# Seven products of halves in place of eight for five more FFN block pairs, with the weight sums made one by one in one buffer

## The chip, the core and the metric

The kernel runs on one core of one Trainium2 chip. The metric is the device time of one execution in microseconds (us); the time before is the median of three runs. One further execution was taken with the hardware profiler, and every duration below is from that one.

Five engines appear in the profile: PE (TensorE, the matmuls, with PEld, its weight loads, shown apart), DVE (VectorE), ACT (ScalarE), POOL (GpSimd) and SP (here only the queue from which transfers are started).

## What is computed

A two-layer decoder trunk for 512 tokens of width 1024: an RG-LRU mixer, a gated conv-FFN, an RWKV-7 mixer, a second conv-FFN and a final norm. The change touches the two FFNs alone. Each computes

```python
def _conv_ffn(x, norm, w_up, conv_w, conv_b, w_down):
    h = _rmsnorm(x, norm)
    u = jnp.einsum('btd,df->btf', h, w_up)              # 512 x 1024 times 1024 x 6144
    gate = _causal_dwconv(u[..., :D_FF], conv_w, conv_b)   # 3 taps, D_FF = 3072
    hid = jax.nn.gelu(gate, approximate=True) * u[..., D_FF:]
    return jnp.einsum('btf,fd->btd', hid, w_down)          # 512 x 3072 times 3072 x 1024
```

All data are float32. The kernel writes each float32 operand as a rounded high part and a low rest and makes every product from three matmuls (high by high, high by low, low by high): this is `mm3`, line 49.

## The kernel before, in words

**Blocks, pairs, stages.** The 3072 hidden channels are 24 blocks of 128, taken in 12 pairs n = 0 to 11. A pair has gate columns G and up columns U, 256 each. Every pair reads four pieces of up weights of 512 KB (512 rows by 256 columns: the upper and the lower half of the rows for G and for U). `ffn` (line 556) goes through the pairs in the order 0, 1, 2, ... After each odd pair from 3 on, `down` (line 784) multiplies four finished hidden blocks with their four pieces of down weights (eight blocks after pair 11). I call an even pair, the odd pair behind it and the down product a *stage*: pairs 2 and 3, 4 and 5, and so on to 10 and 11.

**Two ways to make a pair.** `Whole` (line 665) makes four products, G0, U0, G1, U1: for one half of the rows, 2 column blocks x 4 row blocks x 3 = 24 matmuls with 512 moving columns (all the tokens). `Halves` (line 694) cuts the tokens into two halves of 256 and the rows into two halves, and gets the 2 x 2 block product from seven products in place of eight (Strassen's scheme in Winograd's form). Its products are numbered 1, 5, 6, 2, 7 and then 4, 3; each is 24 matmuls with 256 moving columns. The moving sums (`operands`, line 603) are made once per FFN. The sums of weights are made for each pair, by DVE, in `Halves.weights` (line 698): f[5] = f[7] + f[4], f[6] = f[5] - f[1], f[7] = f[1] - f[7], f[3] = f[6] - f[2], where f[1], f[7], f[4], f[2] are the four pieces as they were loaded.

**Before a product can run**, its weights are split: ACT rounds the piece or sum into a high part (line 93 for Whole and for down pieces, line 711 for Halves) and DVE subtracts (line 96, line 712). A Whole pair has four splits; a Halves pair has seven, and four sums. `ahead` (line 758) keeps the Halves splits two products ahead of the product that is running; `next_weights` (line 177) keeps the other splits two pieces ahead.

**After the products**, results leave the accumulators: for Whole at lines 682 and 688, for Halves at lines 730 (ACT) and 732 to 743 (DVE). `gate` (line 650) applies the convolution (ACT 656, DVE 658 twice for each block) and the gelu (ACT 659); the hidden block is split again (lines 748 to 750, or `split`).

**Which pairs are Halves**: 3, 5, 7, 9, 11 in both FFNs (`HALVES`, line 31). So each of the stages has an even Whole pair and an odd Halves pair.

**Buffers.** All pieces, sums and split parts come from one pool of `N4` = 21 buffers of 4 KB per partition (`b4`, line 83). Eight of them hold the FFN's input in high and low parts (`norm_block`, line 291, through `pair`) for the whole FFN; 13 are left for weights. A buffer is reused when its last reader is done. The framework places every semaphore and, within each engine, may order ready instructions by its own plan, with the written order as the priority; each engine then runs its own list in order.

**Loading.** `weights_load` starts the transfers from SP's queue in the order of the plan (line 99): the up pieces of a stage's pairs, then its four down pieces. They start as buffers come free. For a Halves pair behind a Whole one, line 773 asks for its four pieces just after the even pair's G0.

**Inside a stage** the order on PE is: the even pair; products 1, 5, 6, 2, 7 of the odd pair; the first down piece; products 4 and 3; the second down piece; then `then()`, which calls `ahead` for the next stage; then the third and fourth down pieces together.

Of the kernel before, what the change touches and what calls it, by code (L numbers as in the profile page):

```python
# [7 lines left out]
F32 = mybir.dt.float32  # L8
F32R = mybir.dt.float32r
AF = mybir.ActivationFunctionType  # L10
ALU = mybir.AluOpType
# [16 lines left out]
WARM2 = 20  # L28
WARM = 14

HALVES = (3, 5, 7, 9, 11)

PARAMS = [
    [("lru_b_in", 16), ("lru_conv_w", 32), ("lru_conv_b", 8),
# [9 lines left out]
class Kernel:  # L44
# [54 lines left out]
    def plan_weights(self):  # L99
        I = self.I  # L100
        plan = []
        self.quads = []

        def add(w, r0, c0, k=2, quad=False):
            plan.append((w[r0 : r0 + k * P, c0 : c0 + D // k].rearrange("(k p) c -> p k c", p=P), k, quad))

        def full(w, groups, rows=8):
            for g in groups:
                for k in range(0, rows, 2):
                    add(w, k * P, g * 512)  # L110

        def ffn(l):
            up, dn = I["ffn_w_up"][l], I["ffn_w_down"][l]

            def gu(six):


                for n in range(2 * six, 2 * six + 2):
                    self.quads.append(len(plan))
                    i = int(n in HALVES)  # L120
                    for half, r in ((i, 0), (1 - i, 0), (0, 512), (1, 512)):
                        add(up, r, half * DFF + n * 256, 4, bool(i))

            def dd(row, n):
                for g in range(2):
                    for k in range(0, n, 2):
                        add(dn, row + k * P, g * 512)

            gu(0)
            for six in range(1, 6):  # L130
                gu(six)
                if six < 5:
                    dd((six - 1) * 512, 4)
            dd(2048, 8)

        full(I["lru_w_in"][0], [2, 3, 0, 1])
        full(I["lru_w_out"][0], [0, 1])
        ffn(0)
        for i in (1, 0):
            full(I["rwkv_w_rkv"][0, i], [0, 1])  # L140
        for g in range(4):
            for k in range(0, 8, 4):
                add(I["rwkv_w_rkv"][0, 2], k * P, g * 256, 4)
        for h in range(2):
            for g in range(4):
                add(I["rwkv_w_out"][0], h * 512, g * 256, 4)
        ffn(1)
        self.plan = plan
        self.loaded, self.splitted = {}, {}
        self.n_load = self.n_split = self.n_used = 0  # L150
# [405 lines left out]
    def ffn(self, l, xs, finish, after=None):  # L556
        nc, tc = self.nc, self.tc
        last = l == 1
        with tc.tile_pool(name=f"ffn{l}", bufs=1) as pool:
# [21 lines left out]
            def start(c):  # L581
                if c == 0:
                    norm.append(self.norm_end(rbs))
                    next(norm[0])
                elif c == 1:
                    next(norm[0])
                    if last:
                        self.push(by_tokens())
# [14 lines left out]
            def operands():  # L603
                n1, t2, t3, t4 = sums

                def parts(t, k, f):
                    nc.scalar.copy(t[:, 0, k], f)
                    nc.vector.tensor_tensor(t[:, 1, k], f, t[:, 0, k].bitcast(F32), ALU.subtract)

                stt = nc.vector.scalar_tensor_tensor  # L610
                for k in range(4):
                    x1, x2 = self.x[:, k, :], self.x[:, 4 + k, :]
                    d, f = two(t("s", 7)), two(t("s", 7))
                    nc.scalar.mul(d[:, 0], x1[:, H:], gain(k))
                    stt(d[:, 1], x1[:, 0:H], gain(k), d[:, 0], ALU.mult, ALU.subtract)
                    parts(n1, k, d[:, 1])
                    stt(f[:, 0], x2[:, H:], gain(4 + k), d[:, 1], ALU.mult, ALU.add)
                    parts(t2, k, f[:, 0])
                    stt(f[:, 1], x2[:, 0:H], gain(4 + k), f[:, 0], ALU.mult, ALU.subtract)
                    parts(t4, k, f[:, 1])  # L620
                    stt(d[:, 1], x2[:, H:], gain(4 + k), d[:, 0], ALU.mult, ALU.subtract)
                    parts(t3, k, d[:, 1])
                op = {i: [tuple(part[:, h] for part in xs[k + k0][:2]) for k in range(4)]
                      for i, k0, h in ((1, 0, slice(0, H)), (2, 4, slice(0, H)), (3, 4, slice(H, T)))}
                for i, v in ((5, n1), (6, t2), (7, t3), (4, t4)):
                    op[i] = [(v[:, 0, k], v[:, 1, k]) for k in range(4)]
                return op
# [14 lines left out]
            tt = nc.vector.tensor_tensor  # L642
# [22 lines left out]
            class Whole(Pair):  # L665
                order = (("G0", "U0", "G1", "U1"), ())

                def weights(pair, p):
                    pass
# [24 lines left out]
            class Halves(Pair):  # L694
# [3 lines left out]
                def weights(pair, p):  # L698
                    if p == 1:
                        i = quads[pair.n]  # L700
                        self.weights_load(i + 4)
                        pair.f = dict(zip((1, 7, 4, 2), [self.loaded.pop(i + j) for j in range(4)]))
                    f = pair.f
                    if p == 1:
                        f[5], f[6], f[3] = (self.b4(F32, (4, 256), name) for name in ("S1", "S2", "S4"))
                        tt(f[5], f[7], f[4], ALU.add)
                        tt(f[6], f[5], f[1], ALU.subtract)
                        tt(f[7], f[1], f[7], ALU.subtract)
                        tt(f[3], f[6], f[2], ALU.subtract)
                    hi, lo = self.b4(F32R, (4, 256), f"hi{p}"), self.b4(F32R, (4, 256), f"lo{p}")  # L710
                    nc.scalar.copy(hi, f[p])  # L711
                    tt(lo, f[p], hi.bitcast(F32), ALU.subtract)  # L712
                    pair.w[p] = hi, lo
# [37 lines left out]

            quads = self.quads[l * 12 : l * 12 + 12]
            pairs, hids = {}, []
            kind = lambda n: Halves if n in HALVES else Whole
            seq = [(n, p) for n in range(12) for part in kind(n).order for p in part]
            made, at = [0], [0]

            def ahead(j):
                while made[0] < min(j, len(seq)):
                    n, p = seq[made[0]]  # L760
                    if n not in pairs:
                        pairs[n] = kind(n)(n)
                    pairs[n].weights(p)
                    made[0] += 1

            def products(upto, more=2):

                while True:
                    n, p = seq[at[0]]
                    at[0] += 1  # L770
                    ahead(at[0] + more)
                    pairs[n].product(p)
                    if p == "G0" and n + 1 in HALVES:
                        self.weights_load(quads[n] + 8)
                    if n == 0 and p in ("G0", "U0"):
                        start(int(p == "U0"))
                    if n == 1 and p == "U0":
                        op.update(operands())
                    if p == 7:
                        self.weights_split(quads[n] + 6)  # L780
                    if (n, p) == upto:
                        return
# [57 lines left out]
            for n in range(3, 12, 2):  # L840
                products((n, 7))
                if n == 11 and not last:
                    self.norm_begin()
                    self.push(self.lora_weights())
                down(n, 2 * n - 6, 4 if n < 11 else 8, lambda: products((n, 3)), lambda: ahead(at[0] + 2))
# [879 lines left out]
```

## Time and profile before

| | us |
|---|---|
| median of three runs | 1303.51 (1301.37 to 1304.6) |
| the profiled execution, its own time | 1306.19 |
| its span, first to last instruction | 1304.5 |
| PE busy | 1282.5 |
| DVE busy | 961.5 |
| ACT busy | 666.2 |

The first FFN lies at about 158 to 528 us of the span, the second at about 908 to 1298. In views of the timeline a row gives the start, the length and the instruction (`x24` are 24 merged instructions). In the view by windows each engine has its busy time in that stretch with the count of instructions in brackets; then come the granted TensorE clock, the share of the transfer engines and GB/s. Busy time of PE is of pipelined matmuls whose ends are modelled, so the pace is read from the starts of successive products.

### The profile page before, as it was taken

The numbers are of one execution on the slowest core, as the hardware profiler recorded it, in microseconds if no ns is written. First come the engines' busy times: TensorE is split into PE (matmuls) and PEld (weight loads), VectorE is DVE, ScalarE is ACT, GpSimd is POOL, SyncE is SP. The second block draws the span as 40 slices with busy tenths as digits, with TensorE's granted clock in tenths as the row PEclk, the third lists the DMA queues.
The fourth block names the chain that finished last, engine by engine and source line by source line (L and its number), as shares of the span: only waits on it lengthen the run. The fifth ranks groups of instructions, "written<-read, shape, count | busy, mean of one in ns | idle before, by whom it ended". The sixth has DMA issues, their size and how long they took to land.

```text
span 1304.5 us, 22295 instructions
## 1 busy us (share of the span) xinstructions
PE 1282.5 (98%) x9267; PEld 1077.8 (83%) x9267; DVE 961.5 (74%) x1448; ACT 666.2 (51%) x1064; POOL 67.2 (5%) x114
## 2 busy tenths in 40 slices
PE   9999999999999999999999999899999999999997
PEld 8877888988888888776678788778889898988886
DVE  5988778767667677698889975768777676766754
ACT  6897454433434344468744567655645343433432
POOL 4000000000000000010001121110000000000000
PEclk9999999999999999999899999999999999999999
DMA  6323340515050513422203111222314141505131
GB/s 196 117 65 98 97 134 29 162 33 166 28 177 21 174 50 93 153 65 92 81 23 100 43 53 58 69 83 81 100 62 131 64 146 48 164 31 173 35 132 65
DMA packets 96709, 120.40 MB, mean 92 GB/s; under 512 B 9498, under 2 KB 70628, under 8 KB 96480
## 3 DMA queue, kind: packets, MB, share of 16 engines
q1 hardware_dynamic: 95248, 117.20, 28.5%
q8 instruction: 72, 1.18, 0.4%
q10 hardware_dynamic: 576, 1.05, 0.2%
q0 software_dynamic: 784, 0.74, 0.2%
q14 instruction: 29, 0.24, 0.1%
HBM read 114.44 MB, written 4.52 MB: 91 GB/s over the span
## 4 chain that ended last, share of the span: by engine, by line
PE 87%; DVE 8%; ACT 3%; issue 1%; POOL 0%; POOLq 0%; DVEq 0%; ACTq 0%
PE acc L53 27%; PE accU L53 12%; PE accG L53 12%; PE accA L53 8%; PE accF L53 4%; PE acc L807 3%; PE acc L806 3%; PE acc L805 3%; PE accD L53 2%; PE lg L53 1%; DVE X L1248 1%; DVE wl L96 1%; PE s L1366 1%; PE lwa L53 1%; DVE DA L1246 1%
## 5 line engine op out<-in xcount | busy, mean ns | idle before, releaser
L93 ACT CAST wh<-raw 128x1024 fp32r<-128x1024 f32 (+1 forms) x161 | 166.1, 1043 | 202.9 <-PE acc L53 53.0
L96 DVE TENSOR_TENSOR wl<-raw,wh 128x1024 fp32r<-128x1024 f32 (+1 forms) x161 | 194.3, 1214 | 98.2 <-ACT wh L93 82.9
L53 PE MATMUL accG<-xs,wh 128*128 128x512 f32 x448 | 138.7, 391 | 0.0
L53 PE MATMUL accU<-xs,wh 128*128 128x512 f32 x448 | 138.6, 391 | 0.0
L53 PE MATMUL acc<-hid,wh 128*128 128x512 f32 x384 | 119.7, 395 | 0.0
L53 PEld LDWEIGHTS accG<-xs,wh 128*128 128x128 f32 x448 | 83.7, 188 | 17.3
L53 PEld LDWEIGHTS accU<-xs,wh 128*128 128x128 f32 x448 | 83.6, 188 | 17.1
L53 PE MATMUL accG<-xs,wl 128*128 128x512 f32 x224 | 87.3, 390 | 0.0
L53 PE MATMUL accU<-xs,wl 128*128 128x512 f32 x224 | 87.3, 390 | 0.0
L53 PEld LDWEIGHTS acc<-hid,wh 128*128 128x128 f32 x384 | 71.2, 188 | 16.9 <-ACT wh L93 0.4
L53 PE MATMUL accA<-xt,hi 128*128 128x256 f32 x480 | 83.4, 277 | 0.0
L53 PE MATMUL acc<-xs,wh 128*128 128x512 f32 x256 | 80.2, 394 | 0.0
L658 DVE SCALAR_TENSOR_TENSOR cv<-gpad,pv,cv 128x512 f32<-128x512 f32 x96 | 69.0, 747 | 12.3 <-ACT cv L656 11.8
L712 DVE TENSOR_TENSOR lo<-raw,hi 128x1024 fp32r<-128x1024 f32 x40 | 48.3, 1219 | 40.2 <-PE accU L53 40.2
L807 PE MATMUL acc<-wl,hid 128*128 128x512 f32 (+1 forms) x200 | 77.2, 386 | 0.0
L806 PE MATMUL acc<-wh,hid 128*128 128x512 f32 (+1 forms) x200 | 77.0, 385 | 0.0
L805 PE MATMUL acc<-wh,hid 128*128 128x512 f32 (+1 forms) x200 | 76.7, 383 | 0.0
L53 PE MATMUL acc<-hid,wl 128*128 128x512 f32 x192 | 74.9, 395 | 0.0
L53 PEld LDWEIGHTS accA<-xt,hi 128*128 128x128 f32 x480 | 73.2, 188 | 0.9
L711 ACT CAST hi<-raw 128x1024 fp32r<-128x1024 f32 x40 | 42.0, 1051 | 57.7 <-PE accG L53 49.6
L53 PE MATMUL accA<-xt,lo 128*128 128x256 f32 x240 | 66.3, 276 | 0.0
L53 PE MATMUL acc<-mix,wh 128*128 128x512 f32 x192 | 60.3, 399 | 0.0
(411 smaller groups left out, 3012.9 us busy)
## 6 DMA issues: line engine op xcount, KB each, us to landing
raw<-in_ffn_w_up_dram SPq DMA_DIRECT2D x96, 512.0 KB, 3.6
raw<-in_ffn_w_down_dram SPq DMA_DIRECT2D x48, 512.0 KB, 3.8
raw<-in_rwkv_w_rkv_dram SPq DMA_DIRECT2D x24, 512.0 KB, 3.9
raw<-in_lru_w_in_dram SPq DMA_DIRECT2D x16, 512.0 KB, 3.8
raw<-in_lru_w_out_dram SPq DMA_DIRECT2D x8, 512.0 KB, 3.8
raw<-in_rwkv_w_out_dram SPq DMA_DIRECT2D x8, 512.0 KB, 3.4
xd<-x SPq DMA_DIRECT2D x8, 256.0 KB, 2.1
AR<-xd SPq DMA_DIRECT2D x1, 2048.0 KB, 8.8
```

The costliest lines, as they stand in the source:

```text
L53: mm = lambda *a, **kw: self.nc.tensor.matmul(ps, *a, skip_group_check=more, **kw)
L93: put = (self.nc.vector.tensor_copy if dve else self.nc.scalar.copy)(hi, src)
L96: self.nc.vector.tensor_tensor(lo, src, hi.bitcast(F32), ALU.subtract)
L658: nc.vector.scalar_tensor_tensor(cv, pair.gp[:, e, j : j + T], cw(j), cv, ALU.mult, ALU.add)
L711: nc.scalar.copy(hi, f[p])
L712: tt(lo, f[p], hi.bitcast(F32), ALU.subtract)
L805: nc.tensor.matmul(ps, hh[:, s], wh[:, k, m], start=kk == 0, stop=False)
L806: nc.tensor.matmul(ps, hl[:, s], wh[:, k, m], start=False, stop=False)
L807: nc.tensor.matmul(ps, hh[:, s], wl[:, k, m], start=False, stop=kk == blocks - 1)
L1246: nc.vector.tensor_tensor(w, A[:, s + 1 :, s : s + 1].to_broadcast([P, n, j]), X[:, s : s + 1, 0:j].to_broadcast([P, n, j]), ALU.mult)
L1248: nc.vector.tensor_tensor(X[:, s + 1 :, 0:j], X[:, s + 1 :, 0:j], w, ALU.add)
L1366: nc.tensor.matmul(pss[h][half(z), b, col], w, AR[H][half(h), b, c2, q * P + col.start : q * P + col.stop], start=True, stop=True, tile_po ...
```

## The change

- `HALVES` becomes one set for each FFN. In the first FFN pair 10 becomes a Halves pair. In the second FFN pairs 4, 6, 8 and 10 do, so that all from 3 on are Halves.
- The sums of weights are no longer all made with product 1. f[5] and the new f[7] are made with product 5, f[6] with product 6, f[3] with product 3. f[5], f[6] and f[3] are one buffer ("S"), overwritten in place; three buffers become one.
- The four pieces of an odd Halves pair are asked for after the even pair's product 5, where that is a Halves pair too.
- The first two down pieces are asked for and split after product 7 only where no Halves pair of the same stage follows.

```diff
-HALVES = (3, 5, 7, 9, 11)
+HALVES = ((3, 5, 7, 9, 10, 11), (3, 4, 5, 6, 7, 8, 9, 10, 11))
...
-                    i = int(n in HALVES)
+                    i = int(n in HALVES[l])
...
                     f = pair.f
-                    if p == 1:
-                        f[5], f[6], f[3] = (self.b4(F32, (4, 256), name) for name in ("S1", "S2", "S4"))
+
+                    if p == 5:
+                        f[5] = f[6] = f[3] = self.b4(F32, (4, 256), "S")
                         tt(f[5], f[7], f[4], ALU.add)
+                        tt(f[7], f[1], f[7], ALU.subtract)
+                    if p == 6:
                         tt(f[6], f[5], f[1], ALU.subtract)
-                        tt(f[7], f[1], f[7], ALU.subtract)
+                    if p == 3:
                         tt(f[3], f[6], f[2], ALU.subtract)
...
-            kind = lambda n: Halves if n in HALVES else Whole
+            kind = lambda n: Halves if n in HALVES[l] else Whole
...
-                    if p == "G0" and n + 1 in HALVES:
+                    if p in ("G0", 5) and n + 1 in HALVES[l] and n % 2 == 0:
                         self.weights_load(quads[n] + 8)
...
-                    if p == 7:
+                    if p == 7 and (n % 2 or n + 1 not in HALVES[l]):
                         self.weights_split(quads[n] + 6)
```

## The prediction, made before the changed kernel was timed

> **What bounds the kernel now.** I read the page first: which engine is busy, and on which engine the chain that ended last lies.
>
> ```profile
> span 1304.5 us, 22295 instructions
> PE 1282.5 (98%) x9267; PEld 1077.8 (83%) x9267; DVE 961.5 (74%) x1448; ACT 666.2 (51%) x1064; POOL 67.2 (5%) x114
> PE 87%; DVE 8%; ACT 3%; issue 1%; POOL 0%; POOLq 0%; DVEq 0%; ACTq 0%
> ```
>
> PE is busy for 98% and carries 87% of the chain; but an average can hide stages with other limits. So next the view by windows, cut at the FFNs, and its last window, where PE has nothing to do.
>
> ```profile
> 158.10:528.00 369.90, 369.90 (x2035) 319.93 (x2034) 272.47 (x353) 158.29 (x205) 1.94 (x1) 1.00 0.32 101
> 908.20:1298.00 389.80, 389.46 (x2160) 338.02 (x2159) 262.16 (x338) 163.01 (x221) 4.25 (x5) 1.00 0.30 96
> 1298.00:1304.50 6.50, 0.00 (x0) 0.00 (x0) 1.16 (x4) 1.23 (x3) 0.66 (x1) 0.62 0.22 82
> ```
>
> In both FFNs PE (the first busy figure) is never idle for long, at full clock. Here PE's own work is the time, and only a change of PE's work, or a wait put in front of it, moves the end. The pace is read from the chain in order of time, for pairs 6 and 7 of the second FFN.
>
> ```profile
> 1084.66 5.44 PE accG L53 x24
> 1090.11 5.44 PE accU L53 x24
> 1095.55 5.44 PE accG L53 x24
> 1100.98 5.44 PE accU L53 x24
> 1106.42 2.87 PE accA L53 x24
> 1109.30 2.74 PE accF L53 x24
> 1112.04 2.72 PE accA L53 x24
> 1114.76 2.86 PE accD L53 x24
> 1117.62 2.74 PE accA L53 x24
> ...
> 1125.85 2.75 PE accA L53 x24
> 1128.60 2.86 PE accF L53 x24
> ```
>
> Pair 6 (Whole) takes 4 x 5.44 = 21.76 us of PE. Pair 7 (Halves) takes 2.87 + 2.74 + 2.72 + 2.86 + 2.74 + 2.75 + 2.86 = 19.54 us. No product waits for anything between them.
>
> **The change part by part.** *PE's work.* Five pairs go from Whole to Halves: 5 x (21.76 - 19.54) = 5 x 2.22 = 11.1 us less, all on the path. A half-width matmul starts every 2.74 / 24 = 114 ns and a full one every 5.44 / 24 = 227 ns, so halving costs almost nothing per column, and 7/8 of the work shows as 0.90 of the time.
>
> A rule that speaks against this is in the Trainium skill, page "TensorE: Matmul & The Clock Gate", section "Back-to-back issue gap": with a weight load ahead of each matmul it gives a sustained spacing of about 81 ns at 128 columns and 131 ns at 512. By a straight line between these (an estimate, some 98 ns at 256) a Whole pair would take 96 x 131 ns = 12.6 us and a Halves pair 168 x 98 ns = 16.4 us, and the change would cost 5 x 3.8 = 19 us. The fence above has both products of this kernel timed, at 227 and 114 ns, so the trace decides against that rule and it gets no chance below.
>
> *DVE's work.* What a pair needs, from the groups in the window of that stage (count, busy, mean ns):
>
> ```profile
> L96 DVE TENSOR_TENSOR wl<-raw,wh 128x1024 fp32r<-128x1024 f32 x9 | 11.0, 1223 | 11.6 <-ACT wh L93 7.8 <-PE acc L806 3.7
> L658 DVE SCALAR_TENSOR_TENSOR cv<-gpad,pv,cv 128x512 f32<-128x512 f32 x8 | 5.7, 747 | 0.9 <-ACT cv L656 0.9
> L712 DVE TENSOR_TENSOR lo<-S,hi 128x1024 fp32r<-128x1024 f32 x3 | 3.7, 1222 | 0.3 <-ACT hi L711 0.2
> L709 DVE TENSOR_TENSOR S<-S,raw 128x1024 f32<-128x1024 f32 x1 | 1.2, 1225 | 0.0
> L688 DVE TENSOR_TENSOR s<-accU,ge 128x512 f32<-128x512 f32 x2 | 1.4, 686 | 0.0
> L739 DVE TENSOR_TENSOR gpad<-accA,rb 128x512 f32<-128x512 f32 x1 | 0.7, 692 | 0.7 <-PE accA L53 0.7
> L711 ACT CAST hi<-raw 128x1024 fp32r<-128x1024 f32 x4 | 4.2, 1048 | 6.6 <-PE accG L53 5.8 <-DVE lo L712 0.8
> ```
>
> Whole: 4 splits x 1.22 + 4 x 0.75 (658) + 6 narrow ones x 0.69 = 12.0 us. Halves: 7 splits and 4 sums, 11 x 1.22, + 4 x 0.75 + 9 x 0.69 = 22.6 us. So each changed pair adds 10.6 us to DVE. ACT gains 3 casts of 1.05 and some copies, at half load. Is there room on DVE?
>
> ```profile
> 458.30:528.00 69.70, 69.70 (x386) 60.02 (x386) 53.96 (x66) 31.41 (x40) 0.00 (x0) 1.00 0.30 88
> 1084.70:1148.00 63.30, 63.30 (x361) 55.59 (x360) 42.87 (x51) 24.95 (x30) 0.00 (x0) 1.00 0.32 100
> 180.00:191.00 11.00, 11.00 (x50) 9.12 (x49) 10.93 (x21) 6.12 (x14) 0.00 (x0) 1.00 0.31 98
> 191.00:202.00 11.00, 11.00 (x51) 9.09 (x49) 10.69 (x26) 6.93 (x15) 0.00 (x0) 1.00 0.60 191
> ```
>
> A stage of the second FFN has DVE busy 42.9 of 63.3 us (third busy figure); after, 53.5 of 61.1, 88%. The first FFN's last stage goes from 54.0 of 69.7 to 64.6 of 67.5, 96%. The last two rows show that DVE at 98% does not by itself hold PE, where what it does is not due at once. But inside a stage the load is uneven: the two pairs up to the odd pair's product 7 give DVE 22.6 + 7 splits and sums (8.5) + 3 narrow (2.1) + two down splits (2.4) = 35.6 us in 33.5 us of PE (19.54 + 13.93), of which two products' splits (6 us) are done ahead. About 30 us in 33.5: it fits, with little to spare, and tightest about the end of the even pair, where its gate and hidden work (7 us) meets the odd pair's sums.
>
> *The sums moved.* Same four instructions; two buffers fewer per pair. Sum 6 overwrites sum 5, so on DVE it waits for ACT's cast of sum 5 (1.05) and the split behind it; what is queued behind on DVE is the splits of products 6 and 2. Two products of lead (5.6 us) cover that chain of 1.22 + 1.05 + 1.22 + 1.22 + 1.05 + 1.22 = 7.0 us for two products; without lead it would cost 1.4 us a pair. I take 0 (bounds 0 and 1.4).
>
> *Loads moved.* The odd pair's four loads are asked for at product 5 of the even one; behind them in SP's queue stand the down pieces. The transfers are the same. What may come late is the first down piece, since buffers free up later:
>
> ```profile
> 1111.81 1.23 DVE L712 TENSOR_TENSOR lo<-S,hi 128x1024 fp32r<-128x1024 f32 x1 [0.20 <-ACT hi L711]
> 1112.00 0.37 SPq L157 DMA_DIRECT2D raw<-in_ffn_w_down_dram  x1
> 1115.87 1.05 ACT L93 CAST wh<-raw 128x1024 fp32r<-128x1024 f32 x1 [0.49 <-DMA raw<-in_ffn_w_down_dram]
> 1116.95 1.22 DVE L96 TENSOR_TENSOR wl<-raw,wh 128x1024 fp32r<-128x1024 f32 x1 [3.91 <-ACT wh L93]
> 1120.81 0.37 SPq L157 DMA_DIRECT2D raw<-in_ffn_w_up_dram  x1
> 1125.66 1.05 ACT L93 CAST wh<-raw 128x1024 fp32r<-128x1024 f32 x1 [2.38 <-PE acc L806]
> 1126.74 1.23 DVE L96 TENSOR_TENSOR wl<-raw,wh 128x1024 fp32r<-128x1024 f32 x1 [2.21 <-ACT wh L93]
> 1137.35 1.40 DVE L810 SCALAR_TENSOR_TENSOR xtok<-acc,rs,xtok 128x512 f32<-128x512 f32 x2
> ```
>
> The first load started 5.6 us into the odd pair, when its second product ended and gave a buffer back. Its split was done at 1118.2, 2.2 us ahead of need (1120.4). After, the odd pair's seven splits are made beside its products and no longer ahead of them (before, the last, the first row, was through at 1113.0). By counting the 13 buffers through both pairs I get that load some 2 to 3 us later, so 0 to 0.8 us of waiting a stage, plus what DVE's crowding adds. I take 0.6 us for each of the four stages of the second FFN and 1.2 for the crowded one of the first (bounds 0 and 2.2): 4 x 0.6 + 1.2 = 3.6 us.
>
> *The sum.* 11.1 - 3.6 = 7.5 us less. The profiled execution, 1306.19 us, would be 1298.7; it lies 2.7 above the median 1303.5, so the median becomes 1296.0. About 0.3% (3.9 us) is what a measurement of this kernel can tell from no change.
>
> **The rivals.** *B, DVE becomes the bound at the seam of the two pairs.* From the even pair's product 3 to the odd pair's product 6, 8.5 us of PE, DVE has 7 us of gate and hidden work and splits and sums of products 5 and 6 (three sums and two splits, 6.1 us): 13.1 us. If only two products of lead are there (5.6 us), some 3 us of it spent by ACT's steps in between, the shortfall is 13.1 - 8.5 - 2.6 = 2.0 us a pair. For it: the 88%. Against it: the 7 us can be put off, since these hidden blocks are wanted only by the next stage's down product; and the rows at 98%. Price: of 2.22 won a pair 1.2 to 2.2 are lost, the upper end with the first down piece's wait; 5 x 0.02 to 5 x 1.0 = 0.1 to 5 us are won: 1298.4 to 1303.4.
>
> *C, slower: buffers run out ahead of the fourth down piece.* In the written order `then()` prepares the next even pair ahead of the fourth down piece's split. Before, `then()` had nothing to do (a Whole pair came next) and that split ran at 1126.74, 10 us early, in the two buffers that the first down piece had just left (the cast waits for L806). Now the next pair's four pieces, its first split parts and its sum compete for these: two parts of the third piece, the fourth piece, four up pieces, two parts, a sum, two parts and the two parts in question are 14, and there are 13. If the fourth piece's parts must wait until the second down piece is through, cast 1.05 + split 1.22, and up to four results of DVE in front at 0.70 (1.40 for two), make 5.1 us, of which six matmuls of the third piece (6 x 0.23 = 1.4) are cover: PE waits 0.9 to 3.7 us. It decides from 2.2 us on. Full price: 5 x (3.7 - 2.2) = 7.5 us slower, 1311.0. Against it: the plan is free to split the fourth piece first while the up pieces are still on their way.
>
> For waits this long the Trainium skill (same page, section on the HAM clock gate) says that a window of about 3.4 us without PE work halves the clock; the row of 6.5 us without PE work shows 0.62. By that rule each wait of 3.7 us might cost up to 1.7 us more, and C would end near 1319; my price leaves it out.
>
> *D, the change takes no time from PE* because a Halves pair behind another runs slower. But products 7, 4 and 3 above run behind others of their kind at 2.74 to 2.86 us; at 2.87 for all seven the gain is 1.67 a pair, within the forecast's range. It gets no chance of its own.
>
> **How the numbers follow.** Forecast (11.1 less 0 to 1.2 us a pair, 1292.4 to 1298.4): 0.58. B: 0.24. C: 0.18. Below 1299.6 is faster: all of the forecast and 0.10 of B, 0.68. Within 0.3% (to 1307.4): 0.14 of B and 0.06 of C, 0.20. Slower: 0.12 of C. The range starts at 1291 (no waits at all, less the spread of the runs, 1.5) and reaches to 1306, which leaves out most of C's upper part.
>
> **What would show it.** Right: 15 Halves pairs in place of 10, three copies at L730 and seven casts at L711 for each, the even pairs' products at 2.72 to 2.87 us, a stage of some 61.5 us, PE busy down by about 11, DVE near 53 of 61. B would show as PE waiting for L712 around the seam, C as PE waiting for L96 at the third and fourth down pieces. I am wrong if stages 4 to 10 of the second FFN are longer than 63 us, or if a product of an even Halves pair takes over 3 us without a wait.

## The result: slower, 1325.0 us, and the profile after

The changed kernel takes 1325.03 us (median of 4 runs, 1323.99 to 1326.30) against 1304.05 of the kernel before: a ratio of 1.0169, 95% interval 1.0152 to 1.0185 (the two medians alone give 1.0161). The forecast was 1296.0 (1291 to 1306), so it missed by 29 us and in its sign. The profiled execution is 1325.41 us long, its span 1323.7. In the kernel after, lines from 705 on stand three lower than before (L711 is now L714, L730 is L733, L806 is L809).

The page of the kernel after, span and busy times:

```profile
span 1323.7 us, 23107 instructions
PE 1280.3 (97%) x9627; PEld 1086.9 (82%) x9627; DVE 1006.8 (76%) x1498; ACT 687.4 (52%) x1094; POOL 68.6 (5%) x114
```

VectorE's load rose by 45 us, where 5 x 10.6 = 53 was the forecast. PE's busy time fell by only 2.2 us, not 11, although it does the shorter work. The view by windows says why. Columns are the span of the window, busy time of PE, weight loads, VectorE, ScalarE and GpSimd, the granted clock, DMA share and GB/s:

```profile
158.10:528.00 369.90, 364.41 (x2083) 317.26 (x2083) 276.10 (x356) 158.90 (x207) 1.94 (x1) 1.00 0.31 97
908.90:1317.20 408.30, 392.06 (x2449) 349.44 (x2447) 298.50 (x377) 180.04 (x245) 4.24 (x5) 0.97 0.28 92
1074.44:1077.90 3.46, 0.02 (x1) 0.02 (x1) 3.46 (x5) 1.99 (x2) 0.00 (x0) 1.00 0.00 0
1077.90:1084.70 6.80, 6.35 (x14) 4.58 (x15) 6.12 (x7) 1.61 (x2) 0.00 (x0) 0.50 0.00 0
1146.20:1153.03 6.83, 4.84 (x11) 3.34 (x12) 6.74 (x9) 2.55 (x3) 0.00 (x0) 0.50 0.00 0
1217.88:1224.71 6.83, 5.64 (x14) 4.13 (x13) 5.20 (x6) 2.09 (x2) 0.00 (x0) 0.50 0.00 0
```

The first row is the first FFN, where PE is now idle for 5.5 us (before 0). The second row is the second FFN: before, PE was idle for 0.3 us there at clock 1.00; now it is idle for 16.2 us at clock 0.97. The third and fourth rows are one place of it. PE does nothing for 3.46 us, and for the 6.80 us behind that it runs at a clock of 0.50. Such a wait occurs three times, ending at 1077.9, 1147.8 and 1216.9, and each has one stretch at half clock near its end. The stretches do not begin with the end of the wait each time: the second (fifth row) begins 1.56 us ahead of it, while PE still stands, and the third (last row) 0.94 us behind it. What a stretch costs is half of the time that PE worked in it: (6.35 + 4.84 + 5.64) / 2 = 8.4 us in all. The sum of the second FFN: 16.2 us idle and 8.4 us of lost clock are 24.6 us. From its first product to the end of the span it takes 414.8 us (before 396.4); the clean gain of four pairs, 4 x 2.22, and those 24.6 us give 412.1. The last 2.7 us I can't assign; short waits come out too short, since the ends of matmuls are modelled.

What PE waited for, by the view of waits of the kernel after (us in all, times, longest; one of the five waits of the second row lies ahead of the second FFN, the rest in it):

```profile
PE acc L808 <- ACT wh L93: 11.5, 4, 3.6
PE accA L53 <- ACT s L733: 3.4, 5, 0.7
PE acc L810 <- DVE wl L96: 2.1, 3, 1.2
```

The first row is the third down piece: PE stands at its first matmul until ScalarE has cast it. The last row is its low part, for which PE stands again a few matmuls later; the second row is product 4, which waits for the copy of product 7's result. ScalarE's and then VectorE's timeline ahead of the stop at 1077.90 (start, duration, instruction, in brackets the idle time before it and what ended it):

```profile
1066.70 1.53 ACT L656 ACTIVATE cv<-gpad,pv 128x512 f32<-128x512 f32 x2 [7.57 <-DVE gpad L742]
...
1070.91 1.03 ACT L714 CAST hi<-raw 128x1024 fp32r<-128x1024 f32 x1
1072.23 1.23 ACT L752 CAST hid<-s 128x512 fp32r<-128x512 f32 x2 [0.29 <-DVE s L751]
1075.84 1.04 ACT L714 CAST hi<-S 128x1024 fp32r<-128x1024 f32 x1 [2.38 <-DVE S L707]
1076.79 1.04 ACT L93 CAST wh<-raw 128x1024 fp32r<-128x1024 f32 x1
```

```profile
1073.38 1.21 DVE L715 TENSOR_TENSOR lo<-raw,hi 128x1024 fp32r<-128x1024 f32 x1
1074.51 1.22 DVE L707 TENSOR_TENSOR S<-raw,raw 128x1024 f32<-128x1024 f32 x1
```

The cast of the third piece (L93) needs no input that is late: the four down pieces' loads were all issued by 1057.2. It starts without a gap behind the cast of sum S (L714), and that one has stood for 2.38 us with ScalarE idle, until VectorE had made S. Both belong to the *next* even pair, which PE does not need before 1092.8. So work wanted 15 us later stands ahead, in an in-order queue, of work wanted now. Before, the next pair was Whole there and its pieces came behind.

In the first of the four stages something else decides. There S is ready in time, and ScalarE stands idle ahead of the third piece's cast until PE is through with an earlier piece's matmuls:

```profile
1010.56 1.04 ACT L93 CAST wh<-raw 128x1024 fp32r<-128x1024 f32 x1 [1.42 <-PE acc L809]
```

The cast reads nothing of PE's, so this is a wait for a buffer. PE loses 0.94 us by it. In the other three stages a wait of this kind may be hidden behind the cast of S.

What did come as forecast is the pace of an even halved pair. The chain in order of time, pair 10 of the kernel after:

```profile
1232.37 2.88 PE accA L53 x24
1235.25 2.74 PE accF L53 x24
1237.99 2.72 PE accA L53 x24
1240.71 2.86 PE accD L53 x24
```

### The profile page after: what moved, and what is told of

The parts are those of the page before. It is cut to its first block, busy times and chain, and to the rows that moved or that the text cites. A ratio compares the mean times of both kernels' runs of the same rounds, so it can differ in the third digit from the quotient of the medians.

```text
span 1323.7 us, 23107 instructions
## 1 busy us (share of the span) xinstructions
PE 1280.3 (97%) x9627; PEld 1086.9 (82%) x9627; DVE 1006.8 (76%) x1498; ACT 687.4 (52%) x1094; POOL 68.6 (5%) x114
## 5 line engine op out<-in xcount | busy, mean ns | idle before, releaser
L93 ACT CAST wh<-raw 128x1024 fp32r<-128x1024 f32 (+1 forms) x141 | 144.4, 1041 | 91.8 <-PE acc L53 38.4
L53 PE MATMUL accA<-xt,hi 128*128 128x256 f32 x720 | 127.1, 278 | 3.4 <-ACT s L733 3.4
L53 PEld LDWEIGHTS accA<-xt,hi 128*128 128x128 f32 x720 | 109.4, 188 | 6.0 <-ACT s L733 5.3
L53 PE MATMUL accA<-xt,lo 128*128 128x256 f32 x360 | 99.5, 276 | 0.0
L53 PE MATMUL accG<-xs,wh 128*128 128x512 f32 x288 | 89.4, 392 | 0.0
L53 PE MATMUL accU<-xs,wh 128*128 128x512 f32 x288 | 89.4, 391 | 0.0
L714 ACT CAST hi<-S 128x1024 fp32r<-128x1024 f32 x45 | 47.3, 1050 | 77.3 <-PE accU L53 22.0
L714 ACT CAST hi<-raw 128x1024 fp32r<-128x1024 f32 x60 | 62.8, 1049 | 46.4 <-PE acc L810 18.6
L809 PE MATMUL acc<-wh,hid 128*128 128x512 f32 (+1 forms) x200 | 80.1, 400 | 0.0
L656 ACT ACTIVATE cv<-gpad,pv 128x512 f32<-128x512 f32 x48 | 37.4, 810 | 70.3 <-DVE gpad L742 61.2
L53 PEld LDWEIGHTS accA<-xt,lo 128*128 128x128 f32 x360 | 67.6, 188 | 0.2
L715 DVE TENSOR_TENSOR lo<-S,hi 128x1024 fp32r<-128x1024 f32 x45 | 54.9, 1220 | 13.1 <-ACT hi L714 11.6
L53 PEld LDWEIGHTS accG<-xs,wh 128*128 128x128 f32 x288 | 53.6, 188 | 11.0
```

Of the source, the lines that this page charges most:

```text
L53: mm = lambda *a, **kw: self.nc.tensor.matmul(ps, *a, skip_group_check=more, **kw)
L93: put = (self.nc.vector.tensor_copy if dve else self.nc.scalar.copy)(hi, src)
L656: nc.scalar.activation(cv, pair.gp[:, e, 0:T], AF.Identity, bias=self.vec(f"ffn_conv_b{l}", fb), scale=cw(0))
L809: nc.tensor.matmul(ps, hl[:, s], wh[:, k, m], start=False, stop=False)
```

## The experiments

In each, the ratio is to the kernel before, which ran beside it on the same chip.

### Parts of the change alone

**sums_only**: the sums one by one in one place, and the same ten pairs halved as before.

```diff
-HALVES = ((3, 5, 7, 9, 10, 11), (3, 4, 5, 6, 7, 8, 9, 10, 11))
+HALVES = ((3, 5, 7, 9, 11), (3, 5, 7, 9, 11))
```

> The kernel before with the sums one by one in one buffer, and no more Halves pairs (3, 5, 7, 9, 11 in both FFNs). Order theory and my prediction: no change, within 0.3% of before (1300 to 1308). Rival sums theory: slower by 5 us or more, with PE waiting for L714 or L715.

Measured: 1302.29 us, ratio 1.0003 (0.9990 to 1.0016). The moved sums cost nothing while each pair behind a halved one is Whole; the value 0 taken for them was right.

**first_only**: pair 10 halved in the first FFN alone.

```diff
-HALVES = ((3, 5, 7, 9, 10, 11), (3, 4, 5, 6, 7, 8, 9, 10, 11))
+HALVES = ((3, 5, 7, 9, 10, 11), (3, 5, 7, 9, 11))
```

> The whole change in the first FFN alone (pair 10 Halves there), the second FFN with 3, 5, 7, 9, 11. By the trace of the changed kernel the first FFN ends 5.4 us later than before: 1309 (1307 to 1311) if that delay is carried to the end. Rival: what is late there is caught up in the mixer behind it, 1302 to 1306.

Measured: 1304.9 us, ratio 1.0023 (1.0012 to 1.0034). The rival held in the main. Of the loss of 22 us (1.69%) about 3 come from the first FFN, the rest from the second.

### The order of the down pieces, and the clock

**split_first**: `between()`, the code behind the first down piece, splits the other pieces (the third and fourth) first and only then makes the products 4 and 3 (and with them the next even pair's preparation). Everything else is as after.

```diff
-lambda: products((n, 3))
+lambda: (self.weights_split(self.n_used + 3), products((n, 3)))
```

> The changed kernel, but the third and fourth down pieces of a stage are split ahead of products 4 and 3 of the odd pair, and so ahead of the next even pair's first splits. Order theory (the next pair's splits stand ahead of these pieces' splits on ACT and DVE, PE waits 3.6 us for the third piece and then has half clock for 6.8 us, in three stages of the second FFN): these waits and the half clock go, 3 x (3.6 + 0.4 to 1.2 + 3.4) + 1.1 + 2.2 = 26 us less than 1325, so 1296 to 1302, faster than the kernel before. Rival DVE theory (DVE has too much to do about the seam, whatever the order): the wait only moves to another product, 1318 to 1326. Rival sums theory (the sums in one buffer hold up the chain): 1320 to 1326.

Measured: 1309.54 us, ratio 1.0057 (1.0036 to 1.0079). The waits for down pieces and the half-clock stretches of the second FFN are gone with no buffer added and no work removed: 1.12%, 15 us of the loss of 22. But it is not the 1296 to 1302 that was expected, and a new row heads its waits:

```profile
PE accA L53 <- DVE lo L715: 6.3, 6, 1.7
PE accA L53 <- ACT s L733: 4.7, 8, 0.7
```

**late_both**: another order to the same end. The next even pair's first products are prepared only in `then()`, behind the splits.

```diff
-lambda: products((n, 3)), lambda: ahead(at[0] + 2)
+lambda: products((n, 3), 0), lambda: (self.weights_split(self.n_used + 2), ahead(at[0] + 2))
```

> Here the next even pair's first two products are prepared behind the splits of the third and fourth down pieces, not between them as in the kernel after, and not behind only the last of four as where the down pieces are split first. Theory (order in ScalarE's queue): no wait of PE for the third or fourth down piece in the second FFN, no half-clock stretch there, 1306 to 1311 us. If the order of these splits is all, it comes out like the kernel with all four down pieces split first (1309.5), within 1.5 us. Rival (buffers or VectorE cannot carry two halved pairs in any order): the wait reappears in front of product 1 or 5 of the even pair, 1312 to 1325 us.

Measured: 1309.93 us, ratio 1.0045 (1.0030 to 1.0059), the same as split_first: what mattered is that the splits stand ahead of the next pair's preparation. Both edits put the third and fourth piece ahead in ScalarE's queue and also in the hand-out of the buffers; no run here parts these two effects.

**filler**: the kernel after, order unchanged, with 16 useless matmuls of 512 columns ahead of the third piece in three stages. PE then waits no shorter, but it is not idle meanwhile.

```diff
+if g and not final and n > 3:
+    h = hids[b0][0]
+    for _ in range(16):
+        nc.tensor.matmul(pss[0], h[:, 0:P], h, start=True, stop=True)
```

> The changed kernel with 16 useless matmuls of 512 columns (16 x 0.227 = 3.6 us) put ahead of the third down piece in the three stages of the second FFN that show half clock; the result is overwritten by the next product. If the half clock comes of PE's idle 3.6 us, PE is now busy in that time, the clock stays at 1.00 and 3 x 3.4 us are saved: 1315 (1312 to 1318), though the kernel does more work. If the half clock has another cause, or costs nothing on the path: 1324 to 1327.

Measured: 1316.49 us, ratio 1.0106 (1.0087 to 1.0125). The window that was at 0.50 in the kernel after, here:

```profile
1077.90:1084.70 6.80, 6.55 (x28) 4.92 (x27) 6.35 (x7) 1.55 (x3) 0.00 (x0) 1.00 0.00 0
```

Twice as many matmuls in the same 6.8 us, at clock 1.00. Useless work made the kernel 8.5 us faster, which is the 8.4 us worked out from the three stretches; so of the loss of 22 us about 8.5 is the clock that fell because PE stood still.

### The seam of even and odd pair

split_first still waits 2.1 us for lo in three stages, where an even pair runs into an odd one. Two lines stand out in its timelines, VectorE's and ScalarE's, in front of the wait of 1.68 us at product 7 (1093.8):

```profile
1086.49 1.22 DVE L715 TENSOR_TENSOR lo<-raw,hi 128x1024 fp32r<-128x1024 f32 x1
1091.96 0.69 DVE L735 TENSOR_TENSOR s<-s,accD 128x512 f32<-128x512 f32 x1 [4.25 <-PE accD L53]
1092.56 2.35 DVE L715 TENSOR_TENSOR lo<-raw,hi 128x1024 fp32r<-128x1024 f32 x2
```

```profile
1084.43 1.05 ACT L714 CAST hi<-raw 128x1024 fp32r<-128x1024 f32 x1
1089.09 0.59 ACT L733 COPY s<-accA 128x512 f32<-128x512 f32 x1 [3.60 <-PE accA L53]
1089.58 2.00 ACT L714 CAST hi<-raw 128x1024 fp32r<-128x1024 f32 x2
```

Both engines wait for PE with product 7's parts behind them in their queues. Three causes are possible: a buffer too few, this order, or VectorE's load.

**split_s5**: split_first with one more weight buffer (S in a place of its own, paid for with two copies s).

```diff
-f[5] = f[6] = f[3] = self.b4(F32, (4, 256), "S")
+f[5] = f[6] = f[3] = pool.tile([P, 4, 256], F32, tag="S", name="S", bufs=1)
-s[p] = two(t("s", 7))
+s[p] = two(t("s", 5))
...
```

> The kernel with all four down pieces split first, and one more buffer for weights (the sum S gets a place of its own, two fewer for the products' copies s). Theory that buffers set the seam of even and odd pair: the waits for lo at products 7, 4 and at product 1 of the next pair (1.68 + 0.45 + 0.45 us, three stages, 6.3 in all) go or fall to under 2 us, and the time falls from 1309.5 to 1303 (1302 to 1305.5) us. Rival, VectorE's load sets it: no change, 1308.5 to 1310.5 us. Second rival, the two fewer copies s make a wait of their own: over 1311 us.

Measured: 1308.75 us, ratio 1.0037 (1.0021 to 1.0054). The waits at product 7 are 1.68 us each as before: one buffer more changes nothing.

**split_pin**: split_first with those two places of the order turned round, by pinning three instructions behind what the program issued ahead of them.

```diff
-nc.scalar.copy(hi, f[p])
+(self.tc.keep_in_program_order if p == 7 and l and pair.n % 2 == 0 else lambda i: i)(nc.scalar.copy(hi, f[p]))
...
-nc.scalar.copy(s[p], bank["A"])
+(self.tc.keep_in_program_order if p == 6 and l and pair.n % 2 == 0 else lambda i: i)(nc.scalar.copy(s[p], bank["A"]))
-tt(s[1], s[1], bank["D"], ALU.add)
+(self.tc.keep_in_program_order if l and pair.n % 2 == 0 else lambda i: i)(tt(s[1], s[1], bank["D"], ALU.add))
```

> The kernel with all four down pieces split first, all sums on VectorE, and two places of the order turned round in the even halved pairs of the second FFN: ScalarE casts product 7's weights ahead of the copy of product 6's result, and VectorE makes the lower parts of products 7 and 4 ahead of adding product 2's result. No work less, no buffer more. In the trace of the kernel with all four split first, ScalarE and VectorE stood idle 3.60 and 4.25 us at these two places, with product 7's parts queued behind. Theory that the order alone sets the seam: the wait of 1.68 us at product 7 goes in three stages and what follows it too, 1302 to 1304.5 us. Rival, VectorE has too much to do there: the wait moves to the next products, 1306.5 to 1310 us.

Measured: 1311.42 us, ratio 1.0080 (1.0051 to 1.0109). My theory of the order fell. Product 7 no longer waits, but the chain in order of time now runs through VectorE a few products on:

```profile
1092.24 2.75 PE accA L53 x24
...
1095.65 3.02 PE accA L53 x24
1098.69 0.69 DVE gpad L742
1099.38 1.13 DVE raw L708
1100.52 2.65 DVE cv L658 x4
1103.17 1.14 DVE lo L715
1104.30 0.60 DVE s L746
1104.90 1.20 DVE s L751 x2
1106.10 1.15 DVE S L710
```

VectorE works from 1092 on with hardly a break, and PE gets product 6's parts 1.3 us late. The order only decided where the shortfall shows.

**split_onesum** takes load off VectorE and leaves buffers alone, by leaving out three of four sums in the even pairs of the second FFN.

```diff
+st = tt if pair.n % 2 or not l else lambda *_: None
-tt(f[7], f[1], f[7], ALU.subtract)
+st(f[7], f[1], f[7], ALU.subtract)
...
```

> The kernel with all four down pieces split first; the even halved pairs of the second FFN make only the first of their four sums, and use raw halves and that sum as they are for the other products (three sums of VectorE are left out in each of pairs 4, 6, 8, 10; 3.7 us a pair). Buffers stay as they were. Theory that VectorE's load sets the seam: the 6.3 us of waits for lo go to under 2, 1303 (1302 to 1305.5) us. Rival, buffers set it: the wait of 1.68 at product 7 stays, 1307.5 to 1310.5 us.

Measured: 1299.43 us, ratio 0.9975 (0.9961 to 0.9990). All waits of PE for lo are gone.

**split_gps** does it with nothing left out: the even pairs' sums go to GpSimd.

```diff
+st = nc.gpsimd.tensor_tensor if pair.n % 2 == 0 else tt
-tt(f[5], f[7], f[4], ALU.add)
+st(f[5], f[7], f[4], ALU.add)
...
```

> The kernel with all four down pieces split first; the sums of the even halved pairs are made on GpSimd, which has next to nothing to do in the FFNs. VectorE gets 4.9 us a pair back. If VectorE's load sets the seam and GpSimd's sum takes up to some 2.5 us: 1303 to 1306 us. If buffers set it: 1308 to 1311. Rival: GpSimd's sums are slow (the trace shows none of this size) and products 5 and 7 wait for them, or VectorE slows down beside them: over 1312 us.

Measured: 1298.93 us, ratio 0.9969 (0.9957 to 0.9981): clear of no change, by 0.3%. What two of the four sums cost on GpSimd, by its groups (count, busy, mean ns):

```profile
L708 POOL TENSOR_TENSOR S<-raw,raw 128x1024 f32<-128x1024 f32 x5 | 18.6, 3718 | 505.3 <-DVE cv L658 367.9 <-PE acc L810 93.6 <-DVE s L752 43.9
L711 POOL TENSOR_TENSOR S<-S,raw 128x1024 f32<-128x1024 f32 x5 | 12.0, 2399 | 18.5 <-DVE lo L716 18.5
```

**gps**: the same sums on GpSimd, but with the order of the kernel after.

```diff
-lambda: (self.weights_split(self.n_used + 3), products((n, 3)))
+lambda: products((n, 3))
```

> The kernel after, with nothing changed but the sums of the even halved pairs, which GpSimd makes. The next even pair's preparation still stands ahead of the third and fourth down pieces in ScalarE's queue. Theory (ScalarE's order causes the waits for down pieces, and the half clock behind them): the waits of 3.5 us stay, with 6.8 us at half clock behind each: 1319 to 1328 us. Rival (VectorE's load caused all of it): near 1299, like the kernel with both edits.

Measured: 1341.06 us, ratio 1.0300 (1.0278 to 1.0323): the waits stayed, as the theory had it, and the loss is larger than its range. Its waits, and one window:

```profile
PE acc L809 <- ACT wh L93: 24.7, 7, 5.4
```

```profile
1087.80:1094.60 6.80, 4.80 (x10) 2.98 (x10) 5.67 (x7) 1.81 (x3) 3.29 (x1) 0.50 0.00 0
```

PE waits 5.0 to 5.4 us for the third piece in all four stages (and in three of them 1.2 more for the fourth). The cast of S stands ahead of the third piece in ScalarE's queue as it did, but S is not late here. These rows lead up to the stop that ends at 1089.48 (GpSimd, VectorE, ScalarE); the single row behind them is VectorE at the same place of the kernel after:

```profile
1078.50 2.57 POOL L708 TENSOR_TENSOR S<-raw,raw 128x1024 f32<-128x1024 f32 x1 [42.66 <-PE accF L53]
1081.14 2.73 POOL L709 TENSOR_TENSOR raw<-raw,raw 128x1024 f32<-128x1024 f32 x1
1077.34 7.08 DVE L658 SCALAR_TENSOR_TENSOR cv<-gpad,pv,cv 128x512 f32<-128x512 f32 x4 [0.89 <-ACT cv L656]
1084.46 0.63 ACT L659 ACTIVATE ge<-cv 128x512 f32<-128x512 f32 x1 [2.18 <-DVE cv L658]
1087.44 1.04 ACT L715 CAST hi<-S 128x1024 fp32r<-128x1024 f32 x1
1088.39 1.04 ACT L93 CAST wh<-raw 128x1024 fp32r<-128x1024 f32 x1
```

```profile
1067.55 2.78 DVE L658 SCALAR_TENSOR_TENSOR cv<-gpad,pv,cv 128x512 f32<-128x512 f32 x4 [0.89 <-ACT cv L656]
```

S is made by 1081.07, 6.4 us ahead of its cast. Late is the odd pair's convolution: its four instructions on VectorE take 7.08 us in place of 2.78 while GpSimd makes two sums beside them. The gelu waits for them, and everything behind it in ScalarE's queue moves with it, the third piece last. So this run does not show what the order costs with less load on VectorE, since VectorE was slowed at the place that mattered. It shows how far a delay of one instruction travels through an in-order queue. One edit that gains 0.9% behind the mended order loses 1.3% in front of it.

### Splitting the first piece earlier

**split_gps_d0**: split_gps, and the first down piece is split behind the odd pair's product 6, so that it can stand between products 7 and 4, where PE waited 0.67 us for a copy.

```diff
+if p == 6 and n % 2:
+    self.weights_split(quads[n] + 5)
 if p == 7 and (n % 2 or n + 1 not in HALVES[l]):
```

> The kernel with the down pieces split first and the even pairs' sums on GpSimd (1298.9 us), and the first down piece split already behind the odd pair's product 6, so that its matmuls can stand between products 7 and 4. Theory: the wait of product 4 for the copy of product 7's result (0.67 us of idle time, 0.84 by the pitch, in four stages of the second FFN and one of the first) goes: 1295 (1293 to 1297) us. Rival: the piece takes two of 13 buffers 2.8 us earlier and the odd pair's later parts come late: 1298 to 1302 us.

Measured: 1293.37 us, ratio 0.9937 (0.9916 to 0.9958). PE has no gap over 0.3 us left in the second FFN.

**split_d0**: the same edit, with all sums on VectorE (split_first and the three lines above).

> The kernel with all four down pieces split first (1309.5 us, sums on VectorE), and the first down piece split already behind the odd pair's product 6. Theory that VectorE is full at the seam and that this is a separate cost: the wait of product 4 goes (0.84 us by the pitch in four stages), the waits at the seam stay, 1306 (1304.5 to 1307.5) us. Rival: the piece split earlier puts 1.2 us of VectorE's work in front of the odd pair's last parts, and nothing is won: 1308.5 to 1312 us.

Measured: 1295.79 us, ratio 0.9942 (0.9921 to 0.9963), much better than either theory, and the same as split_gps_d0 within the intervals. The waits at the seam went too, without any load taken from VectorE. The windows of a stage, from product 2 of an even pair to product 2 of the next, first of split_first and then of split_d0:

```profile
1088.89:1154.52 65.63, 62.45 (x434) 57.71 (x433) 51.93 (x60) 29.03 (x36) 0.00 (x0) 1.00 0.30 98
```

```profile
1087.99:1149.48 61.49, 61.49 (x434) 57.38 (x433) 51.63 (x60) 29.01 (x36) 0.00 (x0) 1.00 0.34 109
```

VectorE does the same work in both, 51.9 and 51.6 us. What differs is when it starts. S of the even pair, in split_d0:

```profile
1073.24 1.22 DVE L707 TENSOR_TENSOR S<-raw,raw 128x1024 f32<-128x1024 f32 x1
```

PE begins that pair at 1079.67, so S is 6.4 us ahead of it; in split_first S starts at 1076.95 and PE at 1080.57, 3.6 us. In split_first ScalarE cast the third piece at 1062.50 and the fourth at 1067.79, in split_d0 at 1055.52 and 1064.54, and the next pair's first cast moved forward with them (1072.04 and 1068.78). So the seam needs lead *or* less load: 3 us of lead went with the same effect as 3.7 us of sums taken away. The lead is read from the timelines, not varied by itself. With it the plan's order changed too: in split_d0 ScalarE casts product 7's weights ahead of the copy of product 6's result, and split_pin shows only that this order is not enough alone. A stage of 61.49 us is what the forecast named (some 61.5; 61.1 without any wait).

**split_gps1** and **best1**: split_gps and split_gps_d0 with pair 10 of the first FFN Whole.

```diff
-HALVES = ((3, 5, 7, 9, 10, 11),
+HALVES = ((3, 5, 7, 9, 11),
```

> As the kernel with the down pieces split first and the even pairs' sums on GpSimd (1298.9 us), but with pair 10 of the first FFN Whole, as in the kernel before. In the profile of that kernel the first FFN is 373.1 us long, before 369.7, so the halved pair 10 there loses some 3.4 us, of which the mixer gives part back. Theory: 1296.5 (1295 to 1298) us. Rival, the mixer gives all of it back: 1298 to 1300 us.

> The down pieces split first, the first one already behind the odd pair's product 6, the even pairs' sums on GpSimd (1293.4 us), and pair 10 of the first FFN Whole as before. The first FFN was 371.9 us long with it halved and 369.5 with it Whole. Theory (the loss belongs to the halved pair 10 of the first FFN): 1291 (1289.5 to 1292.5) us. Rival, the mixer gives it back: 1293 to 1295 us.

Measured: 1298.20 us, ratio 0.9973 (0.9960 to 0.9985), and 1294.98 us, 0.9937 (0.9917 to 0.9956). Both times the rival held: the same as with pair 10 halved (0.9969 and 0.9937). Behind the mended order this pair neither gains nor loses what can be measured, though PE does 2.2 us less for it and the first FFN is some 2.4 us longer with it (371.9 against 369.5).

**even0**: best1, with pairs 4, 6 and 8 of the first FFN halved (10 Whole).

```diff
-HALVES = ((3, 5, 7, 9, 11),
+HALVES = ((3, 4, 5, 6, 7, 8, 9, 11),
```

> As best1, with pairs 4, 6 and 8 of the first FFN halved as well (10 Whole). A stage of the first FFN ahead of its last has VectorE busy 45.0 of 64.0 us, and with the sums on GpSimd a halved pair adds some 5.7. Theory (the loss at pair 10 belongs to the last stage, where eight down pieces follow): three pairs at 2.2 us each less than best1, 1284.5 (1283 to 1287) us. Rival (every even halved pair of the first FFN pays, since its hidden work is not the same and its down product waits for PE's evictions): 1290 to 1296 us.

Measured: 1288.42 us, ratio 0.9887 (0.9867 to 0.9907), the fastest of all. Against best1 it is 6.6 us, which looks like three times 2.2. But the profiles of best1 and of even0 put only half of it into the first FFN, from its first product to the last product of pair 11:

```profile
157.87:504.82 346.95, 346.95 (x1936) 301.82 (x1935) 251.65 (x327) 144.72 (x189) 1.94 (x1) 1.00 0.32 99
158.54:502.01 343.47, 341.39 (x2153) 306.82 (x2151) 278.26 (x345) 157.38 (x207) 36.52 (x13) 1.00 0.32 101
```

That is 3.5 us for three pairs; two waits at the seams (1.16 and 0.92 us) take 2.1 of what is missing. The rest of the difference lies in the mixer between the FFNs, where two stretches of 3.41 us ran at half clock in best1 and none in even0. The four runs of best1 were granted a clock of 0.993 to 0.996 over the whole kernel, those of even0 0.995 to 0.999. So these three pairs pay, about half of their price, and the rest of the 6.6 us is clock that the change of the FFN was not shown to cause.

**even0_dve**: even0 with all sums on VectorE.

> As even0 (pairs 4, 6 and 8 of the first FFN halved, 10 Whole, all down pieces split first and the first one behind product 6; 0.9887 of the kernel before), but with every sum on VectorE. Theory that the lead was all that was missing: 1289 (1287 to 1291) us, within 2 us of even0. Rival, VectorE is too full in the first FFN without GpSimd's help (four sums of 1.22 us more in each of three pairs): 1293 to 1298 us, with PE waiting for the lower parts at the seams.

Measured: 1292.07 us, ratio 0.9919 (0.9897 to 0.9940), between the two theories. One row of its waits:

```profile
PE accD L53 <- ACT hi L714: 3.5, 3, 1.2
```

Three waits of 1.2 us at product 2 in the three new stages of the first FFN; even0 has one. The same stretch of the first FFN takes 346.26 us here and 343.47 in even0. So lead is enough in the second FFN, and in the first, with more other work on VectorE, GpSimd's help is worth 2.8 us by these profiles; the intervals of the two ratios touch.

## Why the prediction was wrong

**PE's work** was right in the main: 2.88, 2.74, 2.72 and 2.86 us for an even halved pair's products against 2.87, 2.74, 2.72 and 2.86 worked out. Where nothing waits a stage takes 61.49 us against 63.30 before, so about 1.8 of the 2.22 us are won. The spacings by which the change would have cost time (the Trainium skill, page "TensorE: Matmul & The Clock Gate", section "Back-to-back issue gap") did not hold for these matmuls in any run at full clock.

**VectorE's work** was put too high: 45 us more were measured, not 53. In the working for the stage, "6 us" for two products' splits done ahead counts too much: two splits and two sums of 1.22 us are 4.9. Neither changes the sum.

**The sums moved** at 0: right, as far as sums_only shows it. Two halved pairs in a row with all sums made at product 1 were not run.

**Loads moved** is the step that failed. It took 0.6 us a stage for a first down piece that would come late, and 3.6 us for all waits together. Measured were 5.5 us in the first FFN, 16.2 in the second, and 8.4 of clock, which the sum didn't hold at all: 30.1 us. The part that was forecast is there: product 4 was put ahead of the late piece and waited 0.67 us for a copy in each stage (2.7 us against 2.4; that the size fits is partly luck, since it is another wait), and the earlier split in split_gps_d0 took it away. But the third piece was later: PE waited 0.94, 3.47, 3.59 and 3.47 us for it in the four stages, and in the last three 0.4 to 1.2 more for its low part. I had followed the down pieces through SP's queue and through the buffers, and not through ScalarE's queue. One reading of `products()` was missing for that: it calls `ahead()` two products ahead, so that making products 4 and 3 inside `between()` already issues products 1 and 5 of the next pair, before the third piece's split is issued. The prediction's own sign of being wrong came true: the last three stages of the second FFN, from one product 4 to the next, took 70.0, 69.1 and 70.4 us, not under 63.

**Rival C** was right in kind (PE waits at the late down pieces, up to 3.7 us; measured 3.6) and wrong in place and, for the most part, in cause. It put the next pair's preparation in `then()`, between the third and the fourth piece, and blamed buffers; it stands in `between()`, ahead of both, and split_first removes the wait with no buffer more. In the kernel after, buffers are seen to cost PE time in the first stage alone (0.94 us); how much they add behind ScalarE's queue in the others stays open. C's full price, 1311.0, took off 2.2 us of gain from 3.7 us of wait and left the clock out; the clock decides 8.5 of the 22 us. The sentence on the Trainium skill's rule (page "TensorE: Matmul & The Clock Gate", section on the HAM clock gate: about 3.4 us without work halve the clock) gave 1319 and pointed the right way: half clock came at each stop of 3.5 us, and not where filler kept PE busy. The rule's length does not fit every stop here (see the last section).

**Rival B**, VectorE at the seam, was hidden behind C and real: as soon as the order was mended it cost 6.3 us of waits in three stages. That this is 2.1 us each, and the shortfall worked out was 2.0 us a pair, is partly luck: 1.7 of the 2.1 fall at the even pair's product 7, and only 0.4 to 0.5 at the odd pair's product 6, in the stretch that B named. What was missing there is that the lead is not given: it depends on when the down pieces leave ScalarE's queue, and an earlier split of one piece makes B vanish. The chance of 0.18 for C was too low for a case whose place I had not followed through each engine's queue.

**The first FFN's pair 10**, taken at 1.0 us of gain, lost 2 to 3 us alone and nothing behind the mended order. Which of its last stage's eight down pieces sets it wasn't separated; this stays open.

## What to carry to other kernels

When work is prepared ahead of its time, follow each instruction of it through the in-order queue of *every* engine that it passes, and ask which nearer deadline stands behind it; here a cast wanted 15 us later stood ahead of one wanted at once. When PE will stand still for 3 us or more, count the clock too: here three such waits, 10.5 us, cost another 8.4. Before an engine that is 85% busy in a stage is called too full, look at how early its work may start: here three us of lead went with the same gain as three of its instructions less. Before work is given to GpSimd, look at what VectorE does at that moment.

## What the runs showed of the hardware

- Shorter stops can cost clock as well. In the first FFN's last stage a wait of 1.88 us (split_d0) and of 2.46 us (split_first) was followed by 3.4 us at half clock, while 2.47 us in split_gps and split_onesum, and 1.68 us at the seam of split_first, were not.
- A longer stop need not cost more. Apart from the last few microseconds of the kernel, every stretch at half clock in these traces is 3.41 or 6.83 us long. In gps, one stop of 4.99 us had a stretch of 3.41 us, and three of 5.28 to 5.42 us had 6.83. It begins at no fixed point: up to 1.96 us ahead of the end of the wait (gps), or 1.24 us behind it (split_s5).
- Such stretches come and go in the mixer too, from run to run: the profile of the kernel before has 17.1 us of them there, that of even0 none. Of the 23 runs of the kernel before that ran beside late_both, the slowest took 1306.04 us at a granted clock of 0.992 and the fastest 1299.96 at 0.996. A difference of 2 or 3 us between two kernels can be this alone.
- GpSimd adds two 128x1024 tiles in 2.4 to 3.7 us (means by line, split_gps) where VectorE takes 1.22, and VectorE's instructions beside it can run much longer. Of the 60 splits of lo from raw in split_gps, 11 ran beside a sum of GpSimd and took 1762 ns on average (the longest 3415), the other 49 took 1219. In gps one convolution instruction began 0.22 us behind GpSimd's sum and ended 0.54 us behind that sum's end: 2.89 us in place of 0.75. Instructions that read one operand from the accumulators kept their time (xtok, 743 ns beside a sum and 719 without). The Trainium skill (page "GPSIMD Engine Reference", section "Architecture") says that both share a port to the memory; the trace agrees, since VectorE's instructions ran on past the sum's end.
